# A decoder layer on one core: the opening of its first FFN in an order written out by hand

## The chip, the core and the metric

The kernel runs on one core of one Trainium2 chip. The metric is device time in microseconds (us): the median of the runs of the kernel before is 2044.59 us (three runs, 2043.46 to 2045.07). A core has five engines that run side by side and meet at semaphores: TensorE (PE in the profile; its weight loads are PEld), VectorE (DVE), ScalarE (ACT), GpSimd (POOL) and SyncE (SP), which here issues nearly all transfers. Each engine works through its own queue in order.

## What is computed

One layer with x of 256 tokens by 2048 channels (float32) and a conditioning vector c. Nine vectors of 2048 (shift, scale and gate of three sub-layers) come from c; then an FFN, a token mixer, and a second FFN follow. The change lies in the part that leads to the first products:

```python
mod = (jax.nn.silu(c) @ w_ada[l] + b_ada[l]).reshape(B, 3 * N_SUB, 1, D)
h = modulate(rms_norm(x, g_ffn1[l]), mod[:, 0], mod[:, 1])
x = x + 0.5 * mod[:, 2] * swiglu(h, w_ffn1_gu[l], w_ffn1_down[l])
...
```

`modulate(h, shift, scale)` is `h * (1 + scale) + shift`; `swiglu` takes 5632 gate and 5632 up columns, `silu(g) * u`, and multiplies by `w_down`. `w_ada` is 2048 by 18432, `w_ffn1_gu` 2048 by 11264.

## The kernel before

Tokens lie in two tiles of 128 (`T`), channels in 16 k tiles of 128 (`KD`). A product of float32 quality is made of three float32r products: the activation is split into `hh` and `hl`, the weight into `wh` (ScalarE rounds it, line 180) and `wl` (VectorE subtracts, line 184), and TensorE adds hi*hi, lo*hi and hi*lo (lines 194, 196, 198). The unit of work is a `Set`: 1024 columns of a weight, with four accumulators of 128 by 512 (two token tiles, two column halves) in four of the eight PSUM banks. Two sets in turn use the two groups of four banks; small things use the group that the running set does not hold (`bank`, line 65). A k tile of a set is 12 products. Weights come in transfers of two k tiles (1 MB) into six `raw` buffers; `wh` and `wl` have three buffers each.

The first FFN can't begin before shift and scale of the channels are known. `ada_block` (line 431) makes them for a range of columns: rows of `w_ada` are loaded, each partition sums its rows times silu(c) (VectorE, lines 450 and 452; in a `shared` block every other row goes through TensorE instead, line 448), a product by ones sums over the partitions (line 456), and `mod_col` (line 99) picks the diagonal into columns. The order of the opening (lines 461 to 528) is: c, x in one transfer, then gains and biases in seven small loads on SyncE's queue; a shared block of 256 columns; the first two k tiles; a second shared block of 256; two more; and then three blocks of 512 columns, one while the stretch before it runs. In each of the four stretches of four k tiles (`n`), six sets (`NS`; gate and up columns of the first 3072) run one after the other. At the end of a set's stretch its four accumulators go to `part` in SBUF (ScalarE copies, line 520; later VectorE adds, line 522), so each set is emptied four times. In the last stretch silu and the product of gate and up follow (lines 524, 527). The results are transposed for the down product: `store_T` (line 378) gives four groups of four transposes for each 1024 columns (`pair_T`, line 221), all twelve groups in the next set. `h_tok` (line 285) normalises, transposes and modulates four k tiles of one token tile.

The text lists the work in one order, but the program's scheduler sets each engine's queue anew, by what it holds to be ready. After the opening, `ffn` (line 400) runs the other sets of the first FFN, the first of them the gate of columns 3072 to 4095, with its silu at line 389; side work (`ada_item`, line 115: the other seven vectors) is spread over those sets.

## Time and profile before

| | us |
|---|---|
| median of the runs | 2044.59 |
| span of the profiled execution | 2041.3 |
| TensorE busy | 2008.7 |
| VectorE busy | 1472.2 |
| ScalarE busy | 987.3 |
| bytes read from HBM | 520.00 MB, 256 GB/s over the span |

The profiled execution's time is given as its span, from the first to the last instruction; what lies around it is not in the profile. In the views, a group's row has the line, the engine, the operation, the tiles (out<-in) and shapes, how often it ran, busy us, mean ns of one, and the idle time just before with what ended it. A row of the timeline has the start and the length in us. A row by stretches has the stretch, its length, busy us (and count) of PE, PEld, DVE, ACT and POOL, the granted TensorE clock as a share, the busy share of the transfer engines, and GB/s. TensorE's float32 products with `ones_f`, `cs` or `ident` are entries of several passes, so a count there may be twice that of the text; matmuls are pipelined, so that the distance from start to start and not the length is what one costs.

### The profile page before, as it was taken

How to read it: one execution, taken by the hardware profiler on the slowest of the kernel's cores; microseconds unless marked ns; L12 is line 12 of the kernel's file. 1: busy time of each engine (PE TensorE's matmuls, PEld its weight loads, DVE VectorE, ACT ScalarE, POOL GpSimd, SP SyncE). 2: the span in 40 equal slices, each digit the busy share in tenths (PEclk: the TensorE clock that was granted, in tenths of full speed). 3: DMA queues.
4: the chain of work that ended last, by engine and by line, in shares of the span. 5: the costliest groups of instructions: out<-in, count | busy, mean ns of one | idle time of the engine just before them, and what ended most of it. 6: DMA issues, size and time to landing. Idle time of an engine off the chain costs nothing. (4 is left out here: it accounts for less than half of the span.)

```text
span 2041.3 us, 23823 instructions
## 1 busy us (share of the span) xinstructions
PE 2008.7 (98%) x9053; PEld 1648.5 (81%) x9053; DVE 1472.2 (72%) x1698; ACT 987.3 (48%) x1324; POOL 7.3 (0%) x17
## 2 busy tenths in 40 slices
PE   6999999999999999999999999999999999999999
PEld 4788888888788887888788887788888888888887
DVE  5799878788899956777878788755555555566645
ACT  3554454444544546546554455654443444454443
POOL 0000000000000000000000000000000000000000
PEclk9999999999999999999999999999999999999999
DMA  9988758998898855776868887455655656666762
GB/s 337 356 316 301 279 198 305 334 338 313 318 350 334 333 195 183 252 278 229 293 237 288 292 283 270 165 209 207 243 206 206 228 204 214 219 223 231 233 193 69
DMA packets 157915, 523.69 MB, mean 257 GB/s; under 512 B 9353, under 2 KB 23394, under 8 KB 157544
## 3 DMA queue, kind: packets, MB, share of 16 engines
q1 hardware_dynamic: 157800, 522.16, 72.2%
q8 instruction: 71, 1.16, 0.2%
q14 instruction: 44, 0.36, 0.0%
HBM read 520.00 MB, written 2.12 MB: 256 GB/s over the span
## 5 line engine op out<-in xcount | busy, mean ns | idle before, releaser
L180 ACT CAST wh<-raw 128x1024 fp32r<-128x1024 f32 (+2 forms) x731 | 730.9, 1003 | 949.6 <-PE bank L196 874.2
L184 DVE TENSOR_TENSOR wl<-raw,wh 128x1024 fp32r<-128x1024 f32 (+2 forms) x746 | 842.0, 1136 | 452.2 <-ACT wh L180 447.2
L194 PE MATMUL bank<-wh,hh 128*128 128x512 f32 x2072 | 654.5, 390 | 6.7 <-ACT hh L278 5.7
L198 PE MATMUL bank<-wl,hh 128*128 128x512 f32 x2072 | 651.8, 389 | 0.8 <-DVE wl L184 0.5
L196 PE MATMUL bank<-wh,hl 128*128 128x512 f32 x2072 | 652.1, 389 | 0.0
L194 PEld LDWEIGHTS bank<-wh,hh 128*128 128x128 f32 x2072 | 387.1, 188 | 88.4 <-ACT hh L278 7.8
L198 PEld LDWEIGHTS bank<-wl,hh 128*128 128x128 f32 x2072 | 389.0, 188 | 83.4 <-DVE wl L184 3.9
L196 PEld LDWEIGHTS bank<-wh,hl 128*128 128x128 f32 x2072 | 388.7, 188 | 81.5 <-DVE hl L279 1.4
L129 DVE SCALAR_TENSOR_TENSOR acc<-raw,cs,acc 128x1024 f32<-128x1024 f32 x216 | 276.4, 1279 | 41.2 <-DMA raw<-in_w_ada_dram 39.4
L198 PE MATMUL bank<-wl,sh 128*128 128x512 f32 x692 | 216.9, 390 | 1.9 <-DVE wl L184 1.9
L196 PE MATMUL bank<-wh,sl 128*128 128x512 f32 x692 | 216.6, 390 | 0.3 <-DVE sl L298 0.3
L194 PE MATMUL bank<-wh,sh 128*128 128x512 f32 x692 | 216.7, 390 | 0.0
L198 PEld LDWEIGHTS bank<-wl,sh 128*128 128x128 f32 x692 | 129.7, 188 | 29.6 <-DVE wl L184 2.8
L194 PEld LDWEIGHTS bank<-wh,sh 128*128 128x128 f32 x692 | 129.7, 188 | 28.6 <-ACT wh L180 0.6
L196 PEld LDWEIGHTS bank<-wh,sl 128*128 128x128 f32 x692 | 129.8, 188 | 27.9 <-DVE sl L298 1.0
L452 DVE SCALAR_TENSOR_TENSOR acc<-raw,cs,acc 128x1024 f32<-128x1024 f32 (+1 forms) x59 | 68.1, 1154 | 7.0 <-DMA raw<-in_w_ada_dram 6.2
L298 DVE TENSOR_TENSOR sl<-big,sh 128x512 fp32r<-128x512 f32 x88 | 60.0, 683 | 4.2 <-ACT sh L297 4.2
L297 ACT CAST sh<-big 128x512 fp32r<-128x512 f32 x88 | 54.3, 621 | 8.1 <-DVE big L652 8.1
L522 DVE TENSOR_TENSOR big<-bank,big 128x512 f32<-128x512 f32 x60 | 38.1, 682 | 1.2 <-PE bank L198 0.8
L276 ACT ACTIVATE t<-bank,mcol 128x128 f32<-128x128 f32 x90 | 35.0, 463 | 7.8 <-PE bank L264 7.1
L236 ACT ACTIVATE junk<-x_sb 128x512 bf16<-128x512 f32 x24 | 15.1, 629 | 19.9 <-DVE x_sb L322 13.8
L448 PE MATMUL bank<-raw,cs 128*128 128x256 f32 x64 | 19.4, 458 | 3.3 <-DMA raw<-in_w_ada_dram 3.3
(156 smaller groups left out, 698.2 us busy)
## 6 DMA issues: line engine op xcount, KB each, us to landing
raw<-in_w_ffn_gu_dram SPq DMA_DIRECT2D x176, 1024.0 KB, 5.0
raw<-in_w_ada_dram SPq DMA_DIRECT2D x112, 1024.0 KB, 6.4
raw<-in_w_ffn_down_dram SPq DMA_DIRECT2D x88, 1024.0 KB, 5.8
raw<-in_w_in_dram SPq DMA_DIRECT2D x48, 1024.0 KB, 5.0
raw<-in_w_ada_dram SPq DMA_DIRECT2D x64, 512.0 KB, 7.5
raw<-in_w_o_dram SPq DMA_DIRECT2D x16, 1024.0 KB, 7.1
raw<-in_w_pool_up_dram SPq DMA_DIRECT2D x8, 1024.0 KB, 6.9
raw<-in_w_attn_up_dram SPq DMA_DIRECT2D x8, 1024.0 KB, 5.6
```

The lines of the kernel that those rows point to most:

```text
L129: nc.vector.scalar_tensor_tensor(out=a[0], in0=raw[:, k, :], scalar=sc, in1=a[0], op0=ALU.mult, op1=ALU.add)
L180: nc.scalar.copy(wh, raw_k)
L184: nc.vector.tensor_tensor(wl[:, e], raw_k[:, e], wh[:, e].bitcast(F32), ALU.subtract)
L194: nc.tensor.matmul(self.banks[t][i], hi[:, sl], wh[:, o], start=first, stop=False)
L196: nc.tensor.matmul(self.banks[t][i], lo[:, sl], wh[:, o], start=False, stop=False)
L198: nc.tensor.matmul(self.banks[t][i], hi[:, sl], wl[:, o], start=False, stop=last)
L276: nc.scalar.activation(h[:, f, :], src, AF.Identity, scale=g_, bias=b_)
L297: nc.scalar.copy(hi, src[:, k:k + n, :])
L298: nc.vector.tensor_tensor(lo, src[:, k:k + n, :], hi.bitcast(F32), ALU.subtract)
L448: nc.tensor.matmul(banks[j], sc.to_broadcast([P, P]), r[:, j, :], start=kk == 0, stop=False)
L452: nc.vector.scalar_tensor_tensor(out=acc[0], in0=r, scalar=sc, in1=acc[0], op0=ALU.mult, op1=ALU.add)
L522: nc.vector.tensor_tensor(a, b, a, ALU.add)
```

## The change

The opening stands in a region whose order on every engine is that of the text (`tc.manual_schedule`).

- c and x (two transfers) are loaded first on SyncE; the seven small loads are issued by GpSimd. The transfers of a first block of 256 columns follow, and then the first weights.
- The first block keeps every other row on TensorE, now with `w_ada` as the stationary operand and one column of silu(c) as the moving one, so that sums come out as columns at once (`first_pe`, `ada_col`). The other blocks (256, 256, 512, 512 and 256 columns) are summed by VectorE alone, in pieces of 1 MB at listed places (`blocks`: first k tile, number of k tiles, the pair of each piece, the pair that holds its end).
- Seven sets instead of six: the gate of columns 3072 to 4095 is the seventh. They run in stretches of k tiles `segs`: sets 0 to 5 over k tiles 0 and 1, set 6 over 0 to 5, sets 5 down to 1 over 2 to 5, set 0 over 2 to 9, sets 1 to 5 over 6 to 9, set 6 over 6 to 15, and 5 down to 0 over 10 to 15. The set at a turn goes on without emptying its banks.
- The work is walked through in 56 pairs of k tiles. While pair p is multiplied, pair p + 2 is loaded and pair p + 1 split.
- `Set` can take its banks late, at its first product.
- Scaled x is transposed two k tiles at a time (`x_T`); those of k tiles 2 to 5 are kept in SBUF ahead. Transposes for the down product of two of the three column groups come inside the opening (`turn`), the third after it.

```diff
-NS = 6
+NS = 7
...
-        def __init__(self, w, nk, cols, stat, flip=True):
+        def __init__(self, w, nk, cols, stat, flip=True, late=False):
-            if flip:
+            self.flip, self.banks = flip, None
+            if not late:
+                self.take()
+        def take(self):
+            if self.flip:
                 cur[0] = 1 - cur[0]
             self.banks = [[bank_at(cur[0] * 4 + 2 * t + i, (P, w)) for i, (_, w) in enumerate(self.chunks)]
...
+            if self.banks is None:
+                self.take()
...
-    def ada_block(c0, w, shared):
...
-    nc.sync.dma_start(x_sb, x[0].rearrange("(t p) d -> p t d", p=P))
...
+    order = tc.manual_schedule()
+    order.__enter__()
+    c_row = t_([KD, P], "t2", T2)
+    nc.sync.dma_start(c_row, c[0].rearrange("(k p) -> k p", p=P))
+    for t in range(T):
+        nc.sync.dma_start(x_sb[:, t, :], x[0, t * P:(t + 1) * P, :])
     grow = t_([KG, P], "t2", T2)
     for i, g in enumerate((g_ffn1, g_mix, g_ffn2, pool_scale)):
         n = g.shape[1] // P
-        nc.sync.dma_start(grow[i * KD:i * KD + n, :], g[0].rearrange("(k p) -> k p", p=P))
+        nc.gpsimd.dma_start(grow[i * KD:i * KD + n, :], g[0].rearrange("(k p) -> k p", p=P))
     brow = t_([KB, P], "t2", T2)
     for i in range(3):
-        nc.sync.dma_start(brow[2 * KD * i:2 * KD * (i + 1), :],
...
+        nc.gpsimd.dma_start(brow[2 * KD * i:2 * KD * (i + 1), :],
+                            b_ada[0, 3 * i * D:(3 * i + 2) * D].rearrange("(k p) -> k p", p=P))
+    def ada_load(c0, w, k0):
+        nk = SW // w
+        raw = t_([P, nk, 2, w], "raw", RAW)
+        for j in (1, 0):
+            nc.sync.dma_start(raw[:, :, j, :], ada_v[:, k0:k0 + nk, j * D + c0:j * D + c0 + w])
+        return raw
+    def ada_acc(acc, r, kk, first):
+        sc = cs[:, kk:kk + 1]
+        if first:
+            nc.vector.tensor_scalar_mul(acc, r, sc)
+        else:
+            nc.vector.scalar_tensor_tensor(out=acc, in0=r, scalar=sc, in1=acc, op0=ALU.mult, op1=ALU.add)
+    def ada_col(k, n, j, sums):
+        m = mcol[:, j, k:k + n]
+        if j == 0:
+            nc.vector.tensor_tensor(m, sums, bcol[:, k:k + n], ALU.add)
+        else:
+            nc.vector.scalar_tensor_tensor(out=m, in0=sums, scalar=1.0, in1=bcol[:, KD + k:KD + k + n],
+                                           op0=ALU.add, op1=ALU.add)
+            nc.vector.tensor_tensor(m, m, gcol[:, k:k + n], ALU.mult)
+    def x_T(k, b):
+        xn = t_([P, T, 2 * P], "t2", T2)
+        for t in range(T):
+            nc.scalar.activation(xn[:, t, :], x_sb[:, t, k * P:(k + 2) * P], AF.Copy, scale=st[:, 4, t:t + 1])
+        for f in range(2):
+            for t in range(T):
+                nc.tensor.transpose(b[:, f, t * P:(t + 1) * P], xn[:, t, f * P:(f + 1) * P], ident)
+        return b
+    def h_pair(b, k):
+        h = t_([P, 2, S], "t2", T2)
+        for f in range(2):
+            nc.scalar.activation(h[:, f, :], b[:, f, :], AF.Identity, scale=mcol[:, 1, k + f:k + f + 1],
+                                 bias=mcol[:, 0, k + f:k + f + 1])
+        nc.scalar.copy(hh[:, k:k + 2, :], h)
+        nc.vector.tensor_tensor(hl[:, k:k + 2, :], h, hh[:, k:k + 2, :].bitcast(F32), ALU.subtract)
+    actT = t_([P, KF, S], "big", 1)
+    region = lambda a: actT[:, a:a + 8, :].rearrange("p a b -> p (a b)").rearrange("p (t n) -> p t n", t=T)
+    part = [region(a) for a in (0, 24, 8, 32, 16)] + [t_([P, T, SW], "gate", 1), t_([P, T, SW], "sg", 1)]
+    cols = [(i // 2 * SW + (0 if i % 2 or i == NS - 1 else DFF), SW) for i in range(NS)]
+    xT_sb = actT[:, 40:44, :]
     hh, hl = new_h()
     hstat = lambda k: (hh[:, k, :], hl[:, k, :])
-    actT = t_([P, KF, S], "big", 1)
...
+    segs = [(i, 0, 2) for i in range(6)] + [(6, 0, 6)] + [(i, 2, 6) for i in (5, 4, 3, 2, 1)] + [(0, 2, 10)]
+    segs += [(i, 6, 10) for i in range(1, 6)] + [(6, 6, KD)] + [(i, 10, KD) for i in (5, 4, 3, 2, 1, 0)]
+    pairs = [(n, ka) for n, (i, k0, k1) in enumerate(segs) for ka in range(k0, k1, 2)]
+    def load(p, split=False):
+        n, ka = pairs[p]
+        if n not in sets:
+            sets[n] = Set(w_ffn1_gu[0], KD, cols[segs[n][0]], hstat, late=True)
+        c0, cw = sets[n].cols
+        raws[p] = raw = t_([P, 2, cw], "raw", RAW)
+        src = w_ffn1_gu[0][ka * P:(ka + 2) * P, c0:c0 + cw].rearrange("(k p) n -> p k n", p=P)
+        for k in range(2) if split else [slice(0, 2)]:
+            nc.sync.dma_start(raw[:, k], src[:, k])
+    def prep(p, k):
+        n, ka = pairs[p]
+        items[p, k] = sets[n].prep(ka + k, raws[p][:, k, :])
+    def mm(p, k):
+        n, ka = pairs[p]
+        for t in range(T):
+            sets[n].mm(items[p, k], t, None, segs[n][1], segs[n][2])
+    def evac(p):
+        n, ka = pairs[p]
+        i, k0, k1 = segs[n]
+        if ka + 2 < k1:
+            return
+        for t in range(T):
+            for c_ in range(2):
+                e = slice(c_ * CW, (c_ + 1) * CW)
+                a, b = part[i][:, t, e], sets[n].banks[t][c_]
+                if k0 == 0:
+                    nc.scalar.copy(a, b)
+                else:
+                    nc.vector.tensor_tensor(a, b, a, ALU.add)
+                if k1 == KD:
+                    if i % 2 or i == NS - 1:
+                        nc.scalar.activation(a, a, AF.Silu)
                     else:
-                        nc.vector.tensor_tensor(a, b, a, ALU.add)
...
+                        g = part[i + 1][:, t, e]
                         nc.vector.tensor_tensor(g, a, g, ALU.mult)
-    pend = sum((store_T(part[2 * i], i * SW, SW, actT) for i in range(NS // 2)), [])
+    braw = [ada_load(0, 2 * P, k0) for k0 in (0, 4, 8, 12)]
+    load(0, True)
+    cb = bank_at(4, (P, KD))
+    nc.tensor.transpose(cb, c_row, ident[:KD, :KD])
+    nc.scalar.activation(cs, cb, AF.Silu)
+    bsum = [[bank_at(2 * j + a, (P, 1)) for a in range(2)] for j in range(2)]
+    acc0 = t_([P, 2, 2 * P], "acc", 2)
+    def first_pe(kk, j):
+        for a in range(2):
+            nc.tensor.matmul(bsum[j][a], braw[kk // 4][:, kk % 4, j, a * P:(a + 1) * P], cs[:, kk:kk + 1],
+                             start=kk == 0, stop=False)
+    for k0 in range(0, KD, 4):
+        r = braw[k0 // 4]
+        if k0 < 12:
+            for kk in (k0, k0 + 2):
+                for j in (1, 0):
+                    first_pe(kk, j)
+                ada_acc(acc0, r[:, kk - k0 + 1], kk + 1, kk == 0)
+        else:
+            for j in (1, 0):
+                for kk in (k0, k0 + 2):
+                    ada_acc(acc0[:, j], r[:, kk - k0 + 1, j], kk + 1, False)
+                    first_pe(kk, j)
+                for a in range(2):
+                    nc.tensor.matmul(bsum[j][a], acc0[:, j, a * P:(a + 1) * P], ones_f[:, 0:1], start=False, stop=True)
+                for a in range(2):
+                    ada_col(a, 1, j, bsum[j][a])
+        if k0 < 8:
+            t = k0 // 4
+            for n in range(4):
+                sumsq(t, n)
+            rstd(t)
+            nc.vector.tensor_tensor(st[:, 4, t:t + 1], st[:, 2, t:t + 1], st[:, 3, t:t + 1], ALU.mult)
+        if k0 == 4:
+            for col, row in ((gcol, grow), (bcol, brow)):
+                n = row.shape[0]
+                b = bank_at(4, (P, n))
+                nc.tensor.transpose(b, row, ident[:n, :n])
+                nc.vector.tensor_copy(col, b)
+        if k0 == 8:
+            b0 = x_T(0, bank_at(5, (P, 2, S)))
+            for k in (2, 4):
+                b = x_T(k, bank_at(5 + k // 2, (P, 2, S)))
+                nc.scalar.copy(xT_sb[:, k - 2:k, :], b)
+            load(1)
+            prep(0, 0)
+            prep(0, 1)
+    h = t_([P, 2, S], "t2", T2)
+    for f in range(2):
+        nc.scalar.activation(h[:, f, :], b0[:, f, :], AF.Identity, scale=mcol[:, 1, f:f + 1], bias=mcol[:, 0, f:f + 1])
+        nc.scalar.copy(hh[:, f, :], h[:, f, :])
+        nc.vector.tensor_tensor(hl[:, f, :], h[:, f, :], hh[:, f, :].bitcast(F32), ALU.subtract)
+    blocks = [(2, 2, (0, 1, 2, 3), 5), (4, 2, (4, 5, 6, 6), 7), (6, 4, (8, 9, 10, 11, 12, 13, 15, 16), 18),
+              (10, 4, (17, 19, 20, 21, 22, 24, 25, 26), 28), (14, 2, (28, 30, 31, 32), 35)]
+    for k, n, at, e in blocks:
+        for i, s_ in enumerate(at):
+            pieces.setdefault(s_, []).append((k, n, i))
+        ends[e] = (k, n)
+    def piece_load(k, n, i):
+        araw[k, i] = ada_load(k * P, n * P, i * (SW // (n * P)))
+    def piece(k, n, i):
+        if i == 0:
+            accs[k] = t_([P, 2, n * P], "acc", 2)
+        nk = SW // (n * P)
+        for kk in range(nk):
+            ada_acc(accs[k], araw[k, i][:, kk], i * nk + kk, i + kk == 0)
+    def block_end(k, n):
+        b = bank((P, 2, n))
+        for j in (1, 0):
+            for a in range(n):
+                nc.tensor.matmul(b[:, j, a:a + 1], accs[k][:, j, a * P:(a + 1) * P], ones_f[:, 0:1],
+                                 start=True, stop=True)
+            ada_col(k, n, j, b[:, j, :])
+        for q in range(k, k + n, 2):
+            h_pair(xT_sb[:, q - 2:q, :] if q < 6 else x_T(q, bank((P, 2, S))), q)
+    def turn(p):
+        return store_T(part[2 * p + 1], p * SW, SW, actT)
+    for s_, fs in ((45, turn(2)), (51, turn(1))):
+        for i, f in enumerate(fs):
+            small.setdefault(s_ + i, []).append(f)
+    for q in pieces.get(0, ()):
+        piece_load(*q)
+    for p in range(len(pairs)):
+        if p + 2 < len(pairs):
+            load(p + 2)
+        for q in pieces.get(p + 1, ()):
+            piece_load(*q)
+        if p + 1 < len(pairs):
+            prep(p + 1, 0)
+        mm(p, 0)
+        if p in ends:
+            block_end(*ends[p])
+        for f in small.get(p, ()):
+            f()
+        if p + 1 < len(pairs):
+            prep(p + 1, 1)
+        mm(p, 1)
+        for q in pieces.get(p, ()):
+            piece(*q)
+        evac(p)
+    pend = turn(0)
+    order.__exit__(None, None, None)
```

More of the change, by code (lines that the diff above doesn't have):

```diff
@@ L75, in trunk_layer @@
     nc.vector.tensor_copy(ones, ones_f)
-    c_row = t_([KD, P], "t2", T2)
-    nc.sync.dma_start(c_row, c[0].rearrange("(k p) -> k p", p=P))
-    cb = bank((P, KD))
-    nc.tensor.transpose(cb, c_row, ident[:KD, :KD])
+    x_sb = const.tile([P, T, D], F32, name="x_sb")
+    KG, KB = 3 * KD + PW // P, 6 * KD
+    gcol = const.tile([P, KG], F32, name="gcol")
+    bcol = const.tile([P, KB], F32, name="bcol")
+    psc = gcol[:, 3 * KD:]
     cs = const.tile([P, KD], F32, name="cs")
-    nc.scalar.activation(cs, cb, AF.Silu)
     ada_v = w_ada[0].rearrange("(k p) n -> p k n", p=P)
@@ L425, in ffn @@
         return s
-    x_sb = const.tile([P, T, D], F32, name="x_sb")
-    def ada_block(c0, w, shared):
-        acc, banks = [], []
-        nk = SW // w
-        def f(k0):
-            raw = t_([P, nk, 2, w], "raw", RAW)
-            for j in (1, 0):
-                nc.sync.dma_start(raw[:, :, j, :], ada_v[:, k0:k0 + nk, j * D + c0:j * D + c0 + w])
-            if k0 == 0:
-                banks.extend(bank((P, w)) for _ in range(2))
-                acc.append(t_([P, 2, w], "acc", 2))
-            for kk in range(k0, k0 + nk):
-                sc, r = cs[:, kk:kk + 1], raw[:, kk - k0]
-                if shared and kk % 2 == 0:
-                    for j in range(2):
-                        nc.tensor.matmul(banks[j], sc.to_broadcast([P, P]), r[:, j, :], start=kk == 0, stop=False)
-                elif kk == (1 if shared else 0):
-                    nc.vector.tensor_scalar_mul(acc[0], r, sc)
-                else:
-                    nc.vector.scalar_tensor_tensor(out=acc[0], in0=r, scalar=sc, in1=acc[0],
-                                                   op0=ALU.mult, op1=ALU.add)
-            if k0 + nk == KD:
-                for j in (1, 0):
-                    nc.tensor.matmul(banks[j], ones_f, acc[0][:, j, :], start=not shared, stop=True)
-                    mod_col(j, banks[j], c0)
-        return [lambda k0=k0: f(k0) for k0 in range(0, KD, nk)]
-    nc.sync.dma_start(x_sb, x[0].rearrange("(t p) d -> p t d", p=P))
-    KG, KB = 3 * KD + PW // P, 6 * KD
-    gcol = const.tile([P, KG], F32, name="gcol")
-    bcol = const.tile([P, KB], F32, name="bcol")
+    order = tc.manual_schedule()
[4 more added lines that the diff above has]
+        nc.sync.dma_start(x_sb[:, t, :], x[0, t * P:(t + 1) * P, :])
     grow = t_([KG, P], "t2", T2)
@@ L468, in trunk_layer @@
         n = g.shape[1] // P
-        nc.sync.dma_start(grow[i * KD:i * KD + n, :], g[0].rearrange("(k p) -> k p", p=P))
+        nc.gpsimd.dma_start(grow[i * KD:i * KD + n, :], g[0].rearrange("(k p) -> k p", p=P))
     brow = t_([KB, P], "t2", T2)
     for i in range(3):
-        nc.sync.dma_start(brow[2 * KD * i:2 * KD * (i + 1), :],
-                          b_ada[0, 3 * i * D:(3 * i + 2) * D].rearrange("(k p) -> k p", p=P))
-    for col, row in ((gcol, grow), (bcol, brow)):
-        n = row.shape[0]
-        b = bank((P, n))
-        nc.tensor.transpose(b, row, ident[:n, :n])
-        nc.vector.tensor_copy(col, b)
@@ new lines, in trunk_layer @@
+    pieces, ends, accs, araw = {}, {}, {}, {}
+    for k, n, at, e in blocks:
[10 more added lines that the diff above has]
+            ada_acc(accs[k], araw[k, i][:, kk], i * nk + kk, i + kk == 0)
@@ new lines, in trunk_layer @@
+    small = {}
+    for s_, fs in ((45, turn(2)), (51, turn(1))):
[21 more added lines that the diff above has]
+        evac(p)
```

46 lines of the change are left out of this document (2 added, 44 removed).

## The prediction

> **What bounds the kernel now.** I read the page first, then its slices as stretches of 10 and 20 us, then the timeline of the first 130 us engine by engine, and last the groups of instructions for durations.
>
> ```profile
> span 2041.3 us, 23823 instructions
> ...
> PE 2008.7 (98%) x9053; PEld 1648.5 (81%) x9053; DVE 1472.2 (72%) x1698; ACT 987.3 (48%) x1324; POOL 7.3 (0%) x17
> ```
> ```profile
> 0.00:10.00 10.00, 0.60 (x3) 0.38 (x3) 0.54 (x2) 2.68 (x5) 1.56 (x11) 1.00 0.62 221
> 20.00:30.00 10.00, 7.23 (x31) 4.94 (x30) 6.21 (x14) 1.99 (x2) 0.00 (x0) 1.00 1.08 364
> 40.00:50.00 10.00, 7.25 (x24) 5.40 (x24) 8.18 (x18) 5.29 (x10) 0.00 (x0) 0.83 1.04 396
> 120.00:140.00 20.00, 20.00 (x90) 16.58 (x89) 19.04 (x21) 7.39 (x7) 0.00 (x0) 1.00 0.87 315
> ```
>
> TensorE is busy 98% of the span. Only the first 50 us have holes in its busy time. From 120 us on it is full, with VectorE at 19.0 of 20 us beside it. So the end moves only by what TensorE gains or loses in the opening, and VectorE is the engine that could take over. The rest of the program is the same. I therefore compare one point: the last product of the seventh 1024-column set of the first FFN, with its twelve groups of four transposes done.
>
> ```profile
> 12.31 3.75 PE L448 MATMUL bank<-raw,cs 128*128 128x256 f32 x8 [1.92 <-DMA raw<-in_w_ada_dram]
> 26.98 1.99 ACT L180 CAST wh<-raw 128x1024 fp32r<-128x1024 f32 x2 [10.43 <-DMA raw<-in_w_ffn_gu_dram]
> 31.26 0.73 PE L194 MATMUL bank<-wh,hh 128*128 128x512 f32 x2
> 34.67 5.49 PE L448 MATMUL bank<-raw,cs 128*128 128x256 f32 x24
> 44.05 0.96 PE L194 MATMUL bank<-wh,hh 128*128 128x512 f32 x3 [2.21 <-ACT hh L278]
> 53.07 0.62 PE L196 MATMUL bank<-wh,hl 128*128 128x512 f32 x2
> 53.52 0.61 PE L198 MATMUL bank<-wl,hh 128*128 128x512 f32 x2
> 75.28 0.61 PE L198 MATMUL bank<-wl,hh 128*128 128x512 f32 x2
> 76.42 0.73 PE L194 MATMUL bank<-wh,hh 128*128 128x512 f32 x2 [0.52 <-ACT wh L180]
> 93.86 1.98 PE L456 MATMUL bank<-acc,ones_f 128*128 128x512 f32 x4
> 95.28 1.03 PE L194 MATMUL bank<-wh,hh 128*128 128x512 f32 x2
> 101.15 0.60 PE L264 MATMUL bank<-ident,t 128*128 128x128 f32 x4
> 101.50 0.71 PE L194 MATMUL bank<-wh,hh 128*128 128x512 f32 x2
> ```
> ```profile
> 45.00:46.00 1.00, 1.00 (x5) 0.74 (x4) 0.94 (x4) 0.40 (x2) 0.00 (x0) 0.54 1.02 389
> 46.00:47.00 1.00, 1.00 (x4) 0.81 (x3) 0.96 (x2) 0.42 (x1) 0.00 (x0) 0.50 1.04 387
> 47.00:48.00 1.00, 1.00 (x3) 0.76 (x3) 1.00 (x2) 0.62 (x1) 0.00 (x0) 0.50 1.07 406
> 48.00:49.00 1.00, 1.00 (x5) 0.76 (x4) 0.88 (x1) 0.32 (x1) 0.00 (x0) 0.76 1.04 408
> ```
> ```profile
> 325.48 3.65 PE L225 MATMUL bank<-ident,big 128*128 128x128 f32 x32
> 328.97 1.91 PE L225 MATMUL bank<-ident,sg 128*128 128x128 f32 x16
> 330.64 0.71 PE L194 MATMUL bank<-wh,hh 128*128 128x512 f32 x2
> ```
> ```profile
> L389 ACT ACTIVATE sg<-bank x4: 587/592/598, 362.0 to 364.6; 128x512 f32<-128x512 f32 x4
> ```
>
> Two products take 0.453 us (53.07 to 53.52, and so on through the timeline), 0.2266 us each. A k tile of a set is 12 of them, 2.72 us; a pair of k tiles is 5.44 us; seven sets of 16 k tiles are 1344 products, 304.6 us. The silu of the seventh set starts at 362.0, when its first token tile is closed; the other tile's six products close it at 363.4. So 363.4 - 304.6 = 58.8 us are not products. I can name: the start at 31.3; the second hole, 34.67 to 44.05, 9.4; three sums of a block by ones, 95.28 - 93.86 = 1.4 each, 4.3; six groups of transposes, 0.35 each, 2.1; twelve groups at the end, 330.64 - 325.48 = 5.2; two handovers such as 75.28 + 0.45 to 76.42, 0.7 each, 1.4; the half clock behind the hole, the four stretches of 1 us with 0.54, 0.50, 0.50 and 0.76 as granted clock, 1.7. That is 55.4; of the other 3.4, about 0.9 is side work that already runs in the seventh set (estimate: four sums of 0.23). That side work is only postponed by the change, so the point to beat is 362.5.
>
> **The start.** The new order removes from SyncE's queue seven small loads ahead of the first block, and with them a wait.
>
> ```profile
> SPq L440 <- DMA x_sb<-in_x_dram: 3.8, 1, 3.8
> ```
> ```profile
> 8.75 0.63 ACT L236 ACTIVATE junk<-x_sb 128x512 bf16<-128x512 f32 x1 [5.78 <-DMA x_sb<-in_x_dram]
> ```
> Before, SyncE waits 3.8 us for x to land (8.7) before it issues the first block. After, the block's eight transfers and the first weights follow x directly. x is 2.1 MB; at 364 GB/s that is 5.8 us, so its bytes began at 2.9. x, the 4.2 MB block and 1.05 MB of weights make 7.34 MB, 20.2 us at 364: the weights are in at 23.1, with a little for the last landing 23.6, against 26.98 before. Moving the small loads to GpSimd's queue costs nothing that shows: their transposes stand behind eight products of the block that wait for x and the block's pieces anyway. If they came late, the columns would be late at 27 us, not before.
>
> ```profile
> 125.36 3.60 DVE L184 TENSOR_TENSOR wl<-raw,wh 128x1024 fp32r<-128x1024 f32 x3
> 128.88 2.60 DVE L452 SCALAR_TENSOR_TENSOR acc<-raw,cs,acc 128x1024 f32<-128x1024 f32 x2
> 133.73 2.60 DVE L522 TENSOR_TENSOR big<-bank,big 128x512 f32<-128x512 f32 x4
> 33.25 2.33 DVE L452 SCALAR_TENSOR_TENSOR acc<-raw,cs,acc 128x512 f32<-128x512 f32 x3
> ```
> ```profile
> L180 ACT CAST wh<-raw 128x1024 fp32r<-128x1024 f32 x651 | 684.5, 1055 | 890.7 <-PE bank L196 840.1 <-DMA raw<-in_w_ffn_gu_dram 19.9 <-DVE wl L184 10.8
> L282 ACT CAST hh<-t 128x512 fp32r<-128x512 f32 x18 | 11.4, 633 | 0.2
> L710 ACT ACTIVATE big<-bank,gcol 128x256 f32<-128x256 f32 x8 | 3.8, 473 | 9.0 <-PE bank L707 9.0
> L110 DVE TENSOR_TENSOR mcol<-mcol,bcol 128x4 f32<-128x4 f32 x11 | 1.7, 154 | 0.0
> ```
>
> From these: a low half (L184) takes 1.14 to 1.22, a sum step over 1024 columns 1.26, over 512 columns 0.78, four adds of a set 2.56, a high half 1.05, a 256-wide ScalarE step 0.47, a small column step 0.155. In the hand order VectorE must make both low halves of the first weights before the last quarter of the block. So: weights 23.6, high half 1.05, low half 1.2 (25.9), two 256-column steps 1.0 (estimate, 0.78 less the 0.26 a quarter of the columns is worth), sums 0.4, four column steps 0.6, then the shift half: 1.0, 0.4, 0.3 (29.6), modulation 0.47 and its rounding 0.4, six handovers 0.4: the first product at 30.9. The sums with one column are not in the trace. Lower bound: a load and a pass of a transpose, 5.16 us for 48, 0.108, twice for two passes; upper bound 0.46, two entries of L448 (5.49 for 24). I take the lower, since one column is nearer to 128 than to 256.
>
> **The products.** The second hole goes: the first two k tiles serve six sets one after the other and the seventh runs on to six, nine pairs, 49 us, while the next two blocks arrive. What is late next is the block for k tiles 4 and 5 (`blocks`, second entry). Its last two pieces stand after pair 6 and its end in the middle of pair 7. TensorE meets the block's sums by ones there in its own queue, so it cannot pass them; behind it wait the second half of pair 7 and all of pair 8. Counted from the first product, VectorE until then has: its first free low half at 3.85 (it waits for the third weight buffer, 2.72 + 1.05), 13 halves of 1.14 (14.8), eight pieces of four 512-column steps (two begin with a cheaper one: 24.2), the first block's end 1.2, and 2.2 waiting on ScalarE there and at casts: 46.2. TensorE is there after seven pairs and a half and four small sums: 38.1 + 2.72 + 0.9 = 41.7. It stands 4.5 us. The transfers are not what it waits for: 22 MiB are needed by then, 23.1 MB at 364, 63 + 3 = 66 us against 30.9 + 43 = 74.
>
> From pair 8 to 27 VectorE has 40 halves (45.6), 16 pieces of two steps (40.3) and nine sets' adds (23): 108.9, against 20 x 5.44 = 108.8. It keeps up with nothing to spare; since a set's adds stand ahead of the next halves in its queue, I count 0.9 of lateness in all. The copies of the sets' first sums go to ScalarE, at the 0.59 of the silu row: with two high halves 2.1 + 2.4 of a pair's 5.44, hidden under the next pair's products; without that cover each pair would pay the difference.
>
> Two blocks of four k tiles (ends in pairs 18 and 28) hold a second wait: `x_T` for the second pair of k tiles is copied on ScalarE only after the first pair's modulation and rounding, 0.9 + 0.63 + 0.8 and handovers, some 2.6 us, and TensorE's transposes for it stand ahead of the pair's second half: 5.2 for both. Small things: 28 sums by ones, 6.0 (up to 12.8); five groups of transposes 0.43, 2.2; the twelve groups at the end stay, 5.2. The seam to the automatic order behind pair 55 is taken at nothing, because the next set's halves need only free buffers; if they queue behind the last set's adds and products, it costs four.
>
> **The clock.** Behind 2.21 us of idling TensorE lost 1.7 us at half clock (45 to 49 us above). Its first products of the run are slow too: eight entries of L448 take 3.75 us at 12.31, where 24 of them take 5.49 later. After, it does almost nothing from 20 to 27 us and meets its first products slow: one such stretch or two, 1.7 to 3.4, taken 2.5. The stand of 4.5 costs another 1.7, the two of 2.6 half a chance each, 1.7 together: 5.9.
>
> The Trainium skill, TensorE: Matmul & The Clock Gate, Part 1: The HAM clock gate, says that the clock falls after at least one idle window of about 3.4 us. The rows above speak against the length, since 2.21 us were enough here. By the page the sum would be 1.7 lower.
>
> **The sum.** 30.9 + 304.6 + 5.2 + 6.0 + 2.2 + 4.5 + 0.9 + 5.2 + 5.9 = 365.4, 2.9 after 362.5. The span would be 2044.2. The span shown is 3.3 below the median of the runs (2044.6), so the time is 2047.5. In short: the gain at the start (9.4 of the second hole, its slow clock) is paid back by waits that a fixed order cannot step around.
>
> **Rivals.** Faster: the order holds. If VectorE's steps before pair 7 are 0.1 shorter each, or the sums' wait is short, then the stand and the clock behind all three waits go: 2047.5 - 4.5 - 1.7 - 1.7 = 2039.6. For it: VectorE's margin is counted in tenths over 45 steps. Against: a row of 19.04 of 20 busy shows no such reserve.
>
> Slower: VectorE becomes the bound from pair 8 to 27. If its steps follow each other at their full lengths (1.22, 1.28, 0.68) and not overlapped, its work is 48.8 + 40.0 + 24.5 = 113.3, 4.5 beyond TensorE's; with one more fall of the clock 2053.7. It decides as soon as two pairs cost VectorE over 10.9 us. For it: the strict order leaves gaps at each handover. Against: 125.36 to 136.3 shows the overlap.
>
> By the idle rule: waits of 2.6 us leave the clock alone, which takes the third term of the clock out: 2047.5 - 1.7 = 2045.8. It is the rule of the page of the Trainium skill named above. For it: in the row of before about a microsecond of little work stood beside the 2.21 of idling.
>
> The change does what it says in any case: the order is written out.
>
> **The numbers.** Measuring this kernel tells 0.2% (4.1 us) from no change. Forecast 0.40, own range 2043 to 2052, of it 0.24 within 0.2% and 0.16 slower; order holds 0.32 (0.29 faster, 0.03 same); VectorE 0.21, slower; idle rule 0.07, same. Faster 0.29, same 0.34, slower 0.37. The range, 2036 to 2055, leaves out the low end of the second case and the high end of the third, with the dearer sums and the seam.
>
> **What would show it.** Right: first product at 30 to 32 us; a wait of TensorE for the sum step of VectorE of some 4 us around 75 us, with half-rate products behind it; two waits of 2 to 3 us for ScalarE's scaled copy; the last product of the opening near 364. Wrong: no such wait, or a busy TensorE from 32 us on (then 2040 or less); or several waits for low halves between 90 and 200 us (then over 2052).

## The result, and the profile after

The changed kernel takes 2061.36 us (median of four runs, 2058.87 to 2062.15). The kernel before takes 2044.21 beside it (four runs, 2043.46 to 2045.07). The ratio is 1.0085, with a 95% interval of 1.0071 to 1.01: slower by 17 us. The forecast was 2.9 us slower, and its range ended at 2055.

Two rows of the page after. Span minus span before is 19.1 us (in every run the time is 1.7 to 1.8 above the span, so the profiled execution of before was about 1 us faster than its median, that of after about 1 slower). TensorE's busy time has grown by only 6.5 of it, so most of the loss is TensorE standing still:

```profile
span 2060.4 us, 23934 instructions
...
PE 2015.2 (98%) x9097; PEld 1660.9 (81%) x9097; DVE 1470.0 (71%) x1697; ACT 996.0 (48%) x1327; POOL 10.9 (1%) x24
```

The stretches of 20 us of the kernel after. The columns are those of the view before: busy time of PE, PEld, DVE, ACT and POOL, then the granted clock.

```profile
80.00:100.00 20.00, 15.03 (x56) 12.15 (x55) 13.41 (x18) 7.43 (x11) 0.00 (x0) 0.83 0.72 254
140.00:160.00 20.00, 16.73 (x78) 13.81 (x77) 14.05 (x18) 9.21 (x15) 0.00 (x0) 0.85 0.78 291
160.00:180.00 20.00, 20.00 (x88) 16.49 (x87) 18.21 (x18) 7.53 (x8) 0.00 (x0) 0.98 0.79 280
200.00:220.00 20.00, 17.49 (x85) 14.27 (x85) 15.13 (x18) 8.11 (x12) 0.95 (x1) 0.97 0.76 271
220.00:240.00 20.00, 20.00 (x83) 16.04 (x83) 17.25 (x23) 8.91 (x10) 0.00 (x0) 0.94 0.69 235
```

Before, TensorE was full from 120 us on. Now there are holes at 80, 140 and 200 us, and a low clock beside or behind each. A clock of 0.83 over 20 us is 3.4 us lost; the rows from 80 to 240 us together lose 20 x (0.17 + 0.15 + 0.02 + 0.03 + 0.06) = 8.6.

What TensorE waits for from 36 to 380 us, kernel after (in all, times, longest). `acc` holds a block's sums, `t` of L481 the scaled copy of x, `mcol` a column step; `wl` is a low half and `hh` a rounded activation:

```profile
PE bank L627 <- DVE acc L465: 4.7, 1, 4.7
PE bank L484 <- ACT t L481: 4.3, 2, 2.2
PE bank L627 <- DVE mcol L473: 2.1, 5, 1.1
PE bank L206 <- DVE wl L190: 1.5, 1, 1.5
PE bank L202 <- ACT hh L601: 0.9, 1, 0.9
```

The first two are the waits that the forecast named: a block's sums behind VectorE (4.5 forecast, 4.7 measured), and two waits for the scaled copy (2.6 each forecast, 2.2 each).

The timeline of the kernel after, with the start, the three waits and the end of the opening:

```profile
12.16 6.13 PE L559 MATMUL bank<-cs,raw 128*128 128x1 f32 x28 [0.41 <-DMA raw<-in_w_ada_dram]
22.43 1.95 PE L484 MATMUL bank<-ident,t 128*128 128x128 f32 x8
24.41 0.58 ACT L594 COPY big<-bank 128x512 f32<-128x512 f32 x1 [4.89 <-PE bank L484]
26.79 0.58 ACT L594 COPY big<-bank 128x512 f32<-128x512 f32 x1 [0.99 <-PE bank L484]
27.27 1.99 ACT L186 CAST wh<-raw 128x1024 fp32r<-128x1024 f32 x2
31.69 1.01 PE L575 MATMUL bank<-ones_f,acc 128*128 128x1 f32 x4 [3.43 <-DVE acc L465]
36.18 1.26 PE L202 MATMUL bank<-wh,hh 128*128 128x512 f32 x2 [0.92 <-ACT hh L601]
38.94 1.05 PE L202 MATMUL bank<-wh,hh 128*128 128x512 f32 x2
39.80 1.05 PE L204 MATMUL bank<-wh,hl 128*128 128x512 f32 x2
68.73 0.50 PE L627 MATMUL bank<-ones_f,acc 128*128 128x1 f32 x4
85.81 1.01 PE L627 MATMUL bank<-ones_f,acc 128*128 128x1 f32 x4 [4.72 <-DVE acc L465]
156.19 1.30 PE L484 MATMUL bank<-ident,t 128*128 128x128 f32 x4 [2.17 <-ACT t L481]
389.30 1.91 PE L233 MATMUL bank<-ident,big 128*128 128x128 f32 x16
390.96 0.72 PE L202 MATMUL bank<-wh,hh 128*128 128x512 f32 x2
```

ScalarE stands 4.89 us and then 0.99 for transposes of x, and only at 27.27 does it round the first weights. The first product comes at 36.18, and the next ones lie 0.43 us apart (38.94 to 39.80 is two products, 0.43 each against 0.2266 at full clock), until 41.4 us: 5.2 us at half rate, 2.6 lost. The column of the granted clock shows 1.00 here, because the clock's records in the trace begin only with its first full clock, at 41.4 us.

The last group of sixteen transposes is done at 390.9, where the eighth set has had 48 products. Before, the same group is done at 330.6; with one more set (192 products of 0.2266, 43.5 us) that is 374.1. So 16.8 of the 19.1 us between the spans are lost in the opening. I call 390.9 **the end of the opening** below; a version can be compared at this point, where run times of one kernel lie up to 8 us apart. It comes from one trace of each version, and traces differ by some tenths of a us before the first place where two programs differ (the sums of pair 7 start at 85.81 in the change and at 85.11 in e4, where nothing ahead of them on VectorE is changed). A stretch of half clock can also come out at 3.4 or 6.8 us behind the same wait. Differences of 2 us or less are therefore not shown.

The other 2.3 lie behind it. The two waits for low halves past 1000 us differ by as much. Waits of TensorE from 380 to 1640 us, before and then after:

```profile
PE bank L198 <- DVE wl L184: 2.5, 2, 1.9
```
```profile
PE bank L206 <- DVE wl L190: 4.8, 2, 2.9
```

Of all waits in this stretch only these differ by more than 1 us. Behind the wait of 2.9 stands a stretch of 3.4 us at half clock (1277 us; 1.7 lost) that the trace of before does not have, so the waits are not the whole account of the 2.3.

### The profile page after: what moved, and what is told of

Its sections match the earlier page's. It is cut to its first block, busy times and chain, and to the rows that moved or that the text cites. A ratio compares the mean times of both kernels' runs of the same rounds, so it can differ in the third digit from the quotient of the medians.

```text
span 2060.4 us, 23934 instructions
## 1 busy us (share of the span) xinstructions
PE 2015.2 (98%) x9097; PEld 1660.9 (81%) x9097; DVE 1470.0 (71%) x1697; ACT 996.0 (48%) x1327; POOL 10.9 (1%) x24
## 5 line engine op out<-in xcount | busy, mean ns | idle before, releaser
L465 DVE SCALAR_TENSOR_TENSOR acc<-raw,cs,acc 128x512 f32<-128x512 f32 (+2 forms) x84 | 77.9, 928 | 2.6 <-DMA raw<-in_w_ada_dram 0.6
L390 ACT COPY big<-bank 128x512 f32<-128x512 f32 x44 | 23.2, 594 | 15.4 <-PE bank L233 15.3
L284 ACT ACTIVATE t<-bank,mcol 128x128 f32<-128x128 f32 x60 | 23.3, 461 | 5.4 <-PE bank L272 5.4
```

The source lines that it names most:

```text
L284: nc.scalar.activation(h[:, f, :], src, AF.Identity, scale=g_, bias=b_)
L390: nc.scalar.copy(actT[:, k:k + 2, :].rearrange("p a b -> p (a b)"), b)
L465: nc.vector.scalar_tensor_tensor(out=acc, in0=r, scalar=sc, in1=acc, op0=ALU.mult, op1=ALU.add)
```

## The experiments

On the chips of these runs the kernel before took 2040.5 to 2042.2 us. So the ratios to the kernel before are to be compared with 1.0085, and the ends of the opening with 390.9 (change) and 374.1 (before). By run times alone only e3, e7, e9, e11 and e12 lie clear of the change; the intervals of e1, e2, e4, e5, e8 and e10 overlap its 1.0071 to 1.01, and what these six say rests on one trace each. My theory after the result: an order that is fixed on each engine makes TensorE pay waits that the scheduler's order stepped around, and a half clock behind each. The rivals: VectorE has too much to do whatever the order; or the new division of the work (seven sets, smaller blocks) costs by itself.

**The second transposes earlier (e1).** All of a block's transposes of scaled x are issued at once, before the first modulation:

```diff
+        xs = {q: x_T(q, bank((P, 2, S))) for q in range(max(k, 6), k + n, 2)}
-            h_pair(xT_sb[:, q - 2:q, :] if q < 6 else x_T(q, bank((P, 2, S))), q)
+            h_pair(xT_sb[:, q - 2:q, :] if q < 6 else xs[q], q)
```

> The scaled copies and transposes of both pairs of k tiles stand ahead of the sums by ones in the ends of the two large blocks; nothing else is changed. Waits and clock (my theory): the two stands of 2.17 us for ScalarE's copy go, and with them the half clock behind them (6.8 and 3.4 us at half, 3.4 and 1.7 lost), unless the remaining wait of 1.1 us keeps one: 4.3 to 9.4 us less than 2061.4, so 2052 to 2057. VectorE as the bound from pair 8 to 27 (rival): TensorE only waits elsewhere, within 2 us of 2061.

Measured: 2056.23 us, 1.0076 (1.006 to 1.0091); end of the opening 386.0, 4.9 earlier. The ratio is only 0.0009 (1.8 us) below the change's. Both waits of 2.17 are gone, but TensorE now waits 3.5 us for low halves (waits of TensorE, e1), and the clock drops behind the longer of these:

```profile
PE bank L206 <- DVE wl L190: 3.5, 2, 2.8
```

So mending one wait lets TensorE run into the next thing that is late, and that is VectorE.

At 140 us, however, the clock still drops, with hardly a wait in front of it. A stretch and two rows of the timeline of e1:

```profile
140.00:160.00 20.00, 19.75 (x93) 16.54 (x92) 16.07 (x22) 10.05 (x16) 0.00 (x0) 0.91 0.79 287
150.83 0.95 PE L628 MATMUL bank<-ones_f,acc 128*128 128x1 f32 x8
152.03 1.05 PE L628 MATMUL bank<-ones_f,acc 128*128 128x1 f32 x8 [0.25 <-DVE mcol L473]
```

Half clock lasts from 153.5 to 156.9 us, and in the 6.8 us before it TensorE stood still for 0.25. What stands last there are the transposes and the sixteen one-column entries of the block's sums. In the change the half clock of this place began at 154.08, only 0.06 us into the wait of 2.17 (154.02 to 156.19), so that wait did not bring it on. It lasted 6.8 us there and 3.4 without the wait.

**The second block needed later (e2).** The seventh set stops at k tile 4, and the block for k tiles 4 and 5 ends one pair later:

```diff
-... [(6, 0, 6)] ... [(6, 6, KD)] ...
+... [(6, 0, 4)] ... [(6, 4, KD)] ...
-    blocks = [..., (4, 2, (4, 5, 6, 6), 7), ...
+    blocks = [..., (4, 2, (4, 5, 6, 7), 8), ...
```

> Set 6 turns after four k tiles instead of six, so k tiles 4 and 5 are first needed one pair later, and the second block's last piece and end move one pair back (pieces after pairs 4, 5, 6, 7, end in pair 8). Waits and clock: the stand of 4.72 us and the 6.8 us at half clock behind it (3.4 lost) go: some 8 us less, 2053. VectorE as the bound: the stand only moves to pair 8 or is found again as waits for low halves before pair 28; 2059 to 2061.

Measured: 2057.47 us, 1.0076 (1.0059 to 1.0093); end of the opening 388.8, 2.1 earlier, not the 8 expected. The 4.7 fell to 1.5, but sums of a later block came to wait 2.0 us behind a set's adds in VectorE's queue, and the half clock there, at the same block's sums and its second transposes, lasted 10.2 us. The stretch of e2 (0.85 in the change):

```profile
140.00:160.00 20.00, 15.60 (x67) 12.48 (x66) 12.94 (x18) 7.95 (x13) 0.00 (x0) 0.78 0.60 213
```

**The same work without the fixed order (e3).** Three lines go, and the scheduler orders the queues:

```diff
-    order = tc.manual_schedule()
-    order.__enter__()
-    order.__exit__(None, None, None)
```

> The same text without the region of fixed order, so that the scheduler sets the queues. If the fixed order is what costs (theory), work steps around the waits: 10 to 17 us less, 2044 to 2051. If the content costs (rival: seven sets, four blocks summed on VectorE alone, sums with one column), 2058 or more remain.

Measured: 2046.01 us, 1.0025 (1.0014 to 1.0036); end of the opening 375.7. Waits of TensorE, then a stretch, then the end of the opening in e3:

```profile
PE bank L202 <- ACT hh L490: 2.8, 1, 2.8
PE bank L625 <- DVE acc L463: 2.7, 1, 2.7
```
```profile
80.00:100.00 20.00, 14.23 (x55) 11.45 (x55) 12.89 (x17) 9.50 (x14) 0.00 (x0) 0.83 0.84 292
```
```profile
374.11 1.91 PE L233 MATMUL bank<-ident,big 128*128 128x128 f32 x16
```

15.2 of the 16.8 us in the opening come back with the same instructions on VectorE, 5.4 of them ahead of the first product (30.79). This is the strongest single fact of the study: the order is what the change loses by. It does not say that the new division of the work is free: e3 also has the loads of b1 below, which by themselves are worth 0.2%. The hole at 80 us stays, with its clock; those at 140 and 200 are gone, since the scheduler puts other products ahead of the transposes there.

**TensorE kept busy through the 4.7 us (e4).** Twenty-two idle products before the second block's sums:

```diff
+        if k >= 4:
+            wb = bank()
+            for _ in range({4: 22, 6: 0, 10: 0, 14: 0}[k]):
+                nc.tensor.matmul(wb, hh[:, 0, 0:P], hh[:, 0:2, :].rearrange("p a b -> p (a b)"), start=True, stop=True)
```

> 22 products of 512 columns into a bank that nobody reads stand ahead of the second block's sums by ones, where TensorE otherwise idles 4.72 us; they add 5.0 us of its work and are left out of every sum. If the half clock behind the stand is a cost of its own: 6.8 us at half clock go, 3.4 us less, 0.3 more for the longer filling: some 2058. If the idling alone costs: 2061 to 2062.

Measured: 2055.19 us, 1.0071 (1.0056 to 1.0086); end of the opening 387.5. The timeline and the stretch of e4:

```profile
80.11 5.15 PE L627 MATMUL bank<-hh 128*128 128x512 f32 x22
85.11 0.50 PE L631 MATMUL bank<-ones_f,acc 128*128 128x1 f32 x4
```
```profile
80.00:100.00 20.00, 19.42 (x91) 16.09 (x90) 15.20 (x20) 8.83 (x12) 0.00 (x0) 1.00 0.85 305
```

The wait is as long as it was, the clock is 1.00 where it was 0.83, and the opening ends 3.4 us earlier. The sums come at 85.11 (85.81 in the change), so 2.7 of the 3.4 lie behind them: the clock behind the wait is a cost of its own, over half of the wait.

**The copies of x out of the start (e5), first try.** The transposes for k tiles 2 to 5 go to the tops of pairs 1 and 3:

```diff
-            for k in (2, 4):
-                b = x_T(k, bank_at(5 + k // 2, (P, 2, S)))
-                nc.scalar.copy(xT_sb[:, k - 2:k, :], b)
+        if p in (1, 3):
+            nc.scalar.copy(xT_sb[:, p - 1:p + 1, :], x_T(p + 1, bank((P, 2, S))))
```

> The scaled copies and transposes for k tiles 2 to 5 leave the stretch before the first product and come in pairs 1 and 3; ScalarE then stands free for the first weights' high halves. Start as a cost (theory: ScalarE's queue held them to 27.27 us, while they had landed): first product near 32 to 33 us instead of 36.2, and 3 to 4 us less. Rival, that the pairs behind it are paced by VectorE or by transfers anyway: first product earlier, but the same time within 1.5 us.

Measured: 2060.93 us, 1.01 (1.0082 to 1.0118); end of the opening 391.0. A miss. The first product came at 31.47, 4.7 earlier, but the transposes at their new places wait for ScalarE in the same way (waits of TensorE, e5: four where there were two), and the wait for the sums ends 1 us later:

```profile
PE bank L484 <- ACT t L481: 7.0, 4, 2.2
```

It says nothing on the start by itself; e10 below moves them to a place that costs nothing.

**Half of VectorE's sums left out (e7).**

```diff
-        for kk in range(nk):
+        for kk in range(nk // 2):
```

> VectorE leaves out half of the sum steps of every block but the first (39 us of its work; shift and scale are sums over half the rows). Waits and clock: the wait of 4.72 us for the sums at pair 7, its half clock (3.4) and the waits for low halves (1.5) go, the two for ScalarE's copies with theirs (some 9 us) stay: 9 to 10 us less than the change's 1.0085, a ratio near 1.004. VectorE as the bound of the whole stretch: everything but the start goes, 15 us or more, a ratio of 1.001 or less.

Measured: 2050.54 us, 1.0042 (1.0026 to 1.0058); end of the opening 381.2. Waits of TensorE and two stretches of e7:

```profile
PE bank L484 <- ACT t L481: 4.3, 2, 2.2
PE bank L627 <- DVE acc L465: 0.3, 1, 0.3
```
```profile
140.00:160.00 20.00, 17.57 (x77) 14.38 (x76) 10.89 (x15) 9.77 (x15) 0.00 (x0) 0.83 0.54 193
200.00:220.00 20.00, 17.57 (x80) 14.43 (x78) 11.19 (x17) 10.04 (x15) 0.95 (x1) 0.83 0.57 200
```

The wait for sums is gone with its cause. The other two stay in full though VectorE is busy only 11 of 20 us: they belong to ScalarE's chain and to TensorE's place in its own queue. The kernel is still 0.42% slower than before. VectorE as the bound of the whole is refuted, though 9.7 of the 16.8 us went with half of its sums. The half clock of the second stretch begins at 208.46, 0.04 us into its wait of 2.17, with 0.29 us of standing in the 6.8 us before: as in e1, the block's one-column sums and transposes stand there.

**TensorE kept busy through all waits (e8).** As e4, with 21 products there, ten at each second transpose, and four wide products of `ones_f` before each sum of the first block's scale columns:

```diff
+                for _ in range(4 * j):
+                    nc.tensor.matmul(bank_at(6, (P, 2 * P)), ones_f, braw[0][:, 0, 0, :], start=True, stop=True)
...
+            if n == 4 and q > k:
+                wb = bank()
+                for _ in range(10):
+                    ...
```

> Products that nobody reads fill TensorE's idling ahead of the first block's scale sums (3.4 us), at pair 7 (4.7) and ahead of the second transposes at pairs 18 and 28 (2.2 each); all waits stay. Clock as a cost of its own: full clock at the first product and behind all three stands, 2.6 + 3.4 + 3.4 + 1.7 = 11 us less, a ratio near 1.003. If VectorE paces it anyway: at most 3 us less.

Measured: 2055.55 us, 1.0069 (1.0053 to 1.0085); end of the opening 387.5, not the 11 us earlier that I expected. From 45 us to the end of the opening, half clock was left in one place alone (211.7 us, 3.4 us long, 1.7 lost against 8.6). There TensorE had stood still for 0.27 us in the 6.8 before; it is once more the place of a block's one-column sums. Against the gain, the idle products took 11.0 us (4.9, 2.4 and, at half clock, 3.7) in place of 9.1 of waits, the first product came 1.2 later (37.37), and a low half was now waited for by 1.2. The start stayed slow; the timeline of e8 shows its filling:

```profile
28.20 5.04 PE L575 MATMUL bank<-raw,ones_f 128*128 128x256 f32 x8
```

Eight entries (two for each product) take 0.63 us each, more than the 0.47 of such entries in the slow start of the kernel before (eight in 3.75 us), and the first products behind them were still at half rate. Why the filling did not bring the clock up there stays open.

**No fixed order, and the second block needed later (e9).** e3 and e2 together.

> The automatic order of the third experiment with the second block needed one pair later (as in the second). Waits and clock: the two waits of 2.7 and 2.8 us around that block's end and the 6.8 us at half clock behind it shrink or go: 5 to 9 us less than 1.0025, so 0.998 to 1.000, level with the kernel before or better. VectorE as the bound: no gain beyond 1 us.

Measured: 2045.14 us, 1.002 (1.0011 to 1.003); end of the opening 374.3. A miss: about 1 us less than e3 where 5 to 9 were expected, which is what the rival foretold. The wait for the sums went, the other of e3's two stayed with its half clock (2.83 us from 87.2, and 6.8 us of half clock from 88.1).

**The copies of x out of the start, second try (e10).** The transposes go behind the first products of pair 0, the copies behind the next rounding:

```diff
-            for k in (2, 4):
-                b = x_T(k, bank_at(5 + k // 2, (P, 2, S)))
-                nc.scalar.copy(xT_sb[:, k - 2:k, :], b)
...
+        xb = [x_T(k, bank((P, 2, S))) for k in (2, 4)] if p == 0 else []
...
+        for i, b in enumerate(xb):
+            nc.scalar.copy(xT_sb[:, 2 * i:2 * i + 2, :], b)
```

> As the start experiment, but the scaled copies and transposes for k tiles 2 to 5 lie inside pair 0 where ScalarE and TensorE have nothing to wait for, so that no new stand arises in pairs 1 and 3. Start as a cost of its own: first product near 31.5 us, the end of VectorE's chain at pair 7 earlier by as much, 4 to 5 us less, a ratio near 1.006. If something else paces the first pairs (transfers): within 1.5 us of the change, 1.0085.

Measured: 2055.06 us, 1.007 (1.0054 to 1.0085); end of the opening 385.8, 5.1 earlier. The timeline of e10:

```profile
22.45 1.05 ACT L186 CAST wh<-raw 128x1024 fp32r<-128x1024 f32 x1 [3.92 <-DMA raw<-in_w_ffn_gu_dram]
23.73 1.05 ACT L186 CAST wh<-raw 128x1024 fp32r<-128x1024 f32 x1 [0.23 <-DMA raw<-in_w_ffn_gu_dram]
31.43 1.26 PE L202 MATMUL bank<-wh,hh 128*128 128x512 f32 x2 [0.86 <-ACT hh L598]
81.53 1.01 PE L624 MATMUL bank<-ones_f,acc 128*128 128x1 f32 x4 [4.69 <-DVE acc L465]
```

ScalarE now waits for the weights themselves, and rounds them at 22.45 and 23.73. In the change they had lain there for 3.5 us and more. The wait at pair 7 is still 4.69, so an earlier start moves the whole and doesn't lengthen it.

**No fixed order, second block earlier (e11).** e3, the seventh set to k tile 4 alone, and the block's pieces a pair earlier:

```diff
-    blocks = [..., (4, 2, (4, 5, 6, 6), 7), ...
+    blocks = [..., (4, 2, (3, 4, 5, 6), 7), ...
```

> The automatic order with the second block's four pieces one pair earlier each at the end (after pairs 3, 4, 5, 6, end in pair 7) and k tiles 4 and 5 needed at pair 9. Waits and clock: the 2.7 to 2.8 us of standing near that end and the 6.8 us at half clock behind it go, 5 to 6 us less than 1.0025: 0.999 to 1.000, level with the kernel before. VectorE as the bound: the wait reappears as waits for low halves, 1.002 or more.

Measured: 2044.63 us, 1.0014 (1.0005 to 1.0023); above the 0.999 to 1.000 expected; end of the opening 375.1. Both waits of e3 are gone, and others stand in their place, now for ScalarE's high halves; waits of TensorE, e11:

```profile
PE bank L202 <- ACT wh L186: 4.0, 3, 3.0
```

**All three repairs in the fixed order (e12).** e1, e10, and the segments and pieces of e11.

> The hand order mended at all three places: start as in the run above, second block as in the run beside it, both transposes ahead of the sums in the large blocks. Waits and clock: of the 17 us 4.7 (start), 8.3 (pair 7 with its clock) and 6 to 9 (pairs 18 and 28 with theirs) go, less some 3 us of waits for low halves that appear in their place: a ratio of 0.999 to 1.002. VectorE as the bound: it stays above 1.004.

Measured: 2047.92 us, 1.003 (1.0018 to 1.0041), above the 0.999 to 1.002 expected; end of the opening 377.7, 13.2 of the 16.8 us back. Left are waits for VectorE's column steps and low halves (waits of TensorE, e12), and two half clocks of 3.4 us at 69.9 and 148.4 (the second, at a block's sums, with 1.1 us of standing in the 6.8 before):

```profile
PE bank L625 <- DVE mcol L473: 4.3, 5, 2.9
PE bank L206 <- DVE wl L190: 2.2, 3, 1.0
```

**The start alone, in the kernel before (b1).** x in two transfers and the seven small loads on GpSimd; nothing else of the change:

```diff
-    nc.sync.dma_start(x_sb, x[0].rearrange("(t p) d -> p t d", p=P))
+    for t in range(T):
+        nc.sync.dma_start(x_sb[:, t, :], x[0, t * P:(t + 1) * P, :])
...
-        nc.sync.dma_start(grow[i * KD:i * KD + n, :], g[0].rearrange("(k p) -> k p", p=P))
+        nc.gpsimd.dma_start(grow[i * KD:i * KD + n, :], g[0].rearrange("(k p) -> k p", p=P))
...
-        nc.sync.dma_start(brow[2 * KD * i:2 * KD * (i + 1), :],
+        nc.gpsimd.dma_start(brow[2 * KD * i:2 * KD * (i + 1), :],
```

> The kernel before with only the loads at the start as in the change: x in two transfers, the seven small loads issued by GpSimd, the automatic order kept. If SyncE's wait of 3.8 us for x stood in the first block's way: block and weights land 2 to 3 us earlier, and the first product and the end come 1 to 3 us earlier, 0.9985 to 0.9995. If the transfers' rate paced it: no change.

Measured: 2037.57 us, 0.9979 (0.997 to 0.9988), beside 2042.21 for the kernel before: a little more than the 0.9985 to 0.9995 expected. It is the one version that beats both kernels. Its timeline:

```profile
14.77 3.02 PE L448 MATMUL bank<-raw,cs 128*128 128x256 f32 x12
28.03 0.73 PE L194 MATMUL bank<-wh,hh 128*128 128x512 f32 x2
40.78 0.96 PE L194 MATMUL bank<-wh,hh 128*128 128x512 f32 x3 [2.21 <-ACT hh L278]
325.71 1.91 PE L225 MATMUL bank<-ident,sg 128*128 128x128 f32 x16
```

The first product comes at 28.03 instead of 31.26 and the same transposes end 3.3 us earlier: the gain of the start is kept to the end. The second hole is still there.

b1 also bears on the rival that the new division of the work costs by itself. e3 has the same loads and the scheduler's order, and differs from b1 by the new division: 1.0025 against 0.9979, some 9 us slower, 4.9 of them in the opening (375.7 against 327.3 + 43.5 = 370.8). So that rival is right in part; its cost is hidden behind the gain of the loads when e3 is set against the kernel before alone.

## Why the prediction was wrong, step by step

Most of the mechanisms were right and in their places; two terms of the sum, the start and the clock, were mis-sized by 5 us each. At the forecast's own point (365.4; measured 390.9 less the 48 products of the eighth set, 10.9, so 380.0) it is 14.6 us short:

- **The start, 30.9 forecast, 36.18 measured: the first step that failed, 5.3 us.** The transfers were right: the weights are there at 23.7 (e10), 23.6 forecast. What I left out is what stands ahead of their rounding in ScalarE's queue. Two copies of x wait for transposes that stand in TensorE's queue behind the first block's one-column products, and these run at 0.22 us an entry (28 entries in 6.13 us), of which the sum of the start has none. So the rounding began at 27.27 and not at 23.6. The forecast asked what stands ahead in the queues of SyncE and GpSimd, and did not ask it of ScalarE's. e10 shows it: with the copies moved, the start gives back 4.75 and the opening 5.1. The rest, 27.27 to 36.18, is 8.9 against the 7.3 of the forecast, with its sums at half rate (four entries in 1.01 us at 31.69, 0.50 at 68.73).
- **The clock, 5.9 forecast, 11.2 measured (2.6 + 8.6): the second step that failed, 5.3 us.** I took 1.7 for each stretch of half clock, from the one stretch of 3.4 us that the trace before shows, and gave the two waits for the copy only half a chance each. The start's share was right (2.5 forecast, 2.6 measured); the rest was 8.6 against 3.4. At each wait of 2 us or more in the opening stood a stretch of half clock, two of them 6.8 us long. e4 and e8 show the term apart from the waits. But the tie to the waits, which the forecast took for granted, holds only in part: at the ends of the large blocks half clock came with 0.25 to 0.29 us of standing (e1, e7, e8). The one-column sums and transposes stand in front of it each time; that they bring it on is not shown, since no run took them away.
- **The waits.** The one at pair 7 was 4.72 (4.5), those for the scaled copy 2.17 at the transposes and 3.3 and 2.4 with all that is beside them (2.6 each), low halves 1.5 (0.9). In all, TensorE stands 12.8 us between the first product and the end of the opening, against 10.6 (4.5, 0.9 and 5.2): 2.2. The 4.5 came out by two errors that cancel: counted from the first product, TensorE was at the sums after 44.9 us (41.7 forecast) and VectorE done with them after 49.6 (46.2). Both are some 3.3 late; the 2.6 of the slow start delays both, which is argued and not tried alone.
- **Sums by one column, 6.0 forecast.** The four entries at 68.73 take 0.50 with the tail of the last, and start 0.11 us apart, so 56 are 6.2: the choice of the lower bound was right. About 1.6 us of the 14.6 is not assigned.
- **The seam** cost nothing, as forecast: TensorE has no wait at the change from the hand order to the scheduler's. The small loads on GpSimd cost nothing either, and b1 shows them as part of a gain.

Of the rivals, VectorE as the bound is wrong as a whole (e3, e7), but right in small places: each repair (e1, e2, e8, e12) brought out waits for VectorE, 1.2 to 4.3 us, that another wait had covered. This fits that the repairs give less together than the sum of their terms: 4.9, 5.1 and up to 8 us for the third (4.7 of wait and 3.4 of clock), 13.2 together. The order that holds did not come true. The idle rule of the Trainium skill, TensorE: Matmul & The Clock Gate, Part 1: The HAM clock gate, would have left the clock alone behind waits of 2.2 us. The rows speak against it: the clock is 0.83 in two stretches of 20 us in e7, in each of which TensorE stands 2.43 us altogether.

The sentence under the forecast's sum, that the gain is paid back by waits that a fixed order cannot step around, has the right sign, and the cause is right as far as the order goes (e3). The gain was the second hole of 9.4, and it did go. What was paid for it was 14.6 more than counted, a third of it ahead of the first product, which came 4.9 us later than before where I had counted on 0.4 earlier.

What stays open: the start's clock in e8, and the cost behind the opening. The versions without the fixed order end their openings within 0.2 to 1.6 us of 374.1 and are still 0.14 to 0.25% slower than the kernel before. In e3 some 2 us of that stand in the same two late waits for low halves, with 3.4 us of half clock behind them; waits of TensorE from 380 to 1640 us, e3:

```profile
PE bank L206 <- DVE wl L190: 4.4, 2, 2.8
```

They are not a mark of the seven sets: over the versions with seven sets they come to 1.2 (e4), 3.1 (e1) and up to 5.9 us (e9), against 2.5 before, and e1, e4 and e5 have no half clock there. Why they vary no run tried, and with one trace of each version it cannot be told from scatter.

## What to carry to other kernels

An order written by hand turns each wait on its path into a stop of TensorE, and most stops of 2 us or more came with a stretch of half clock; price both, and look also at what little work stands beside a stop, since half clock came here with almost no stop at all. Before trusting the order run the same work with the scheduler's, which here gave back 12 of 17 us. For a chain that ends in the first product, write down what stands ahead of each step in every engine's queue, the engines that only copy included. Try the parts of a large change alone: the smallest part of this one, in the old order, was worth 0.2% by itself.

## What the runs showed of the hardware

- Half clock comes in lengths of 3.4, 6.8 and once 10.2 us (e2). Before, one wait of 2.21 was followed by 3.4 us. The length of a wait does not decide it: behind waits of 1.90 us (change, at 1031) and 2.40 (e5, at 1271) the clock stayed full.
- Half clock also came with almost no wait: 0.25 us of standing in the 6.8 us before it in e1, 0.27 in e8, 0.29 in e7, each time at a block's sixteen one-column entries.
- Products with one moving column did not bring the clock up: 0.22 us an entry from 12 to 22 us, and the first products at 36.18 still at half rate. Products with 256 columns did in b1, though not as the filling of e8: in b1 twelve entries from 14.77 take 3.02 us, 0.25 each, near the 0.23 of full clock (24 in 5.49, before), and the clock's records begin with full clock at 14.5 us, against 41.4 in the change.
- A float32 product with one column costs 0.11 us an entry from start to start at full clock and 0.21 at half (four entries take 0.50 and 1.01 us with the tail of the last), about as much as a transpose's 0.108.
